# Three of six additions into the residual, from DVE to adding transfers on POOL's queue

## The chip, the cores and the metric

The kernel runs on one core of a Trainium2 chip. The metric is the device time of one execution in microseconds. The core's engines appear as PE (matrix multiplications), DVE (element-wise work on two tensors), ACT (element-wise functions of one tensor), POOL (a second, general engine) and SP (here it only issues transfers). They run side by side and wait for each other through semaphores. Tiles lie in SBUF, 128 partitions wide; matmul results arrive in eight PSUM banks.

## The reference, cut to what matters

Two decoder layers over 256 positions and a model width of 2048, in float32. A layer adds a mixer's output and then a gated feed-forward to the residual:

```
x = x + concatenate([main, mo]) @ w_out[l]
x = x + conv_ffn(rmsnorm(x, g_ffn[l]), w_ffn_up[l], conv_w[l], conv_b[l], w_ffn_down[l])
...
return rmsnorm(x, g_final)

def conv_ffn(h, w_up, cw, cb, w_down):
    a = h @ w_up
    c = causal depthwise convolution of a, width 3, plus cb
    gate, val = c[..., :D_FF], c[..., D_FF:]
    return (silu(gate) * val) @ w_down
```

The inner width D_FF is 5632. What is changed lies in the last line: the product with `w_down` and its addition to the residual.

## The kernel before

**Splits.** Each float32 operand of a matmul is split into a rounded high part and a remainder: ACT writes `whi` (L118 for `w_up`, L709 for `w_down`), DVE writes `wlo` (L119, L710), and PE adds three matmuls per product (L157, L158, L160 for `w_up`, L795 to L797 for `w_down`). Weights come in pieces of 512 KB, issued by SP into four `raw` buffers; `whi` has four buffers, `wlo` five.

**The feed-forward** of a layer runs in three parts of 4, 4 and 3 groups of 512 inner columns. In a part, each group has a gate product and a value product over 16 blocks of the model width (eight chunks each); then two down phases, `ph` 0 and 1, multiply the part's result by `w_down` for the left and the right 1024 output columns. Tokens lie along partitions there: `xt` is the residual, 128 partitions x 2 token blocks x 2048 columns.

**The fast scheme.** Some chunks of a down phase use seven instead of eight block products (a Strassen-like scheme on 2 token blocks x 2 column halves of 512). Four of the products, m1, m5, m6 and m7, have accumulators of their own; the others go straight into the plain accumulators e00, e01, e10, e11. After the last fast chunk, `between` (L1386, ACT) copies the four into a `staged` tile, [128, 2, 4, 512], one set per phase. The plain accumulators are added to `xt` by DVE in `added` (L1407).

**The combine** (`combine`, L1391) later makes the four outputs of the staged products with six DVE operations: two on `staged` itself and four additions or a subtraction into `xt`. For the two phases of the first and second part it is deferred to chunks 2 and 5 of the next part's first gate product. In the third part only phase 0 is fast, and its combine comes right after the first accumulator is added, at the start of phase 1. So a layer has five combines, the program ten.

**Who reads next.** After a deferred combine, `xt` is touched next by the additions of the next part's accumulators. After the last combine of layer 0 (class `Inner`), the additions of e01, e10 and e11, ACT's squares (L1430) and PE's transposes of the first 1024 columns (L406, from `turned`) follow during phase 1; the transposed residual reuses the memory of `staged`. In layer 1 (class `Last`) the additions, the squares (L1499) and the multiplications by the final gain (L1504) follow, and DVE's queue then holds the last weight splits.

**Order.** A scheduler of the framework fixes each engine's order ahead of the run from its own estimates of durations. `keep_in_program_order` holds marked instructions of one engine in the order of the code. The rows of `between` and `combine` follow their data dependences.

Of the kernel before, what the change touches and what calls it, by code (L numbers as in the profile page):

```python
# [13 lines left out]
ALU = mybir.AluOpType  # L14
AX = mybir.AxisListType

P = 128
# [1322 lines left out]
class Tokens:  # L1340
# [48 lines left out]
    def combine(self, ph):  # L1389
        xt, m = self.xt, self.staged[:, ph]  # L1390
        tt = lambda *a: self.k.tc.keep_in_program_order(self.nc.vector.tensor_tensor(*a))  # L1391
        n1, n2 = (slice((2 * ph + i) * 512, (2 * ph + i + 1) * 512) for i in range(2))
        tt(m[:, 2], m[:, 2], m[:, 0], ALU.subtract)
        tt(m[:, 3], m[:, 3], m[:, 2], ALU.add)
        tt(xt[:, 0, n1], xt[:, 0, n1], m[:, 0], ALU.add)
        tt(xt[:, 1, n1], xt[:, 1, n1], m[:, 3], ALU.subtract)
        tt(xt[:, :, n2], xt[:, :, n2], m[:, 1:2].to_broadcast([P, 2, 512]), ALU.add)
        tt(xt[:, :, n2], xt[:, :, n2], m[:, 2:4], ALU.add)

    def deferred(self):  # L1400
        waiting, self.waiting = self.waiting, []
# [155 lines left out]
```

## Time and profile before

| | |
|---|---|
| Median of three runs | 2030.46 us (2029.62 to 2032.41) |
| Profiled execution: span, first to last instruction | 2027.8 us |
| Granted PE clock, mean | 0.999 |
| PE busy | 2017.2 us, 15136 matmuls |
| DVE busy | 1618.2 us, 2433 instructions |
| ACT busy | 1167.1 us |
| POOL busy | 112.8 us |
| Transfers | 409.24 MB, 202 GB/s on average |
| Additions into `xt` by combines (L1391) | 40, from 614.9 to 1997.2 us |

The page gives the profiled execution's span, not its time with what lies around it; the span is 2.7 us below the median of the runs. A row of a timeline gives the start in us, the duration of the merged instructions, engine, line, operation, the tiles written and read, the count, and in brackets the engine's idle time just before and what ended it. A row of a group gives count, then busy us and mean ns, then idle time and its releaser. A row of a window gives, after its length, each engine's busy time with its instructions, then the granted clock, the share of the DMA engines' time that was busy, and GB/s.

### The profile page before, as it was taken

The numbers are of one execution on the slowest core, as the hardware profiler recorded it, in microseconds if no ns is written. First come the engines' busy times: TensorE is split into PE (matmuls) and PEld (weight loads), VectorE is DVE, ScalarE is ACT, GpSimd is POOL, SyncE is SP. The second block draws the span as 40 slices with busy tenths as digits, with TensorE's granted clock in tenths as the row PEclk, the third lists the DMA queues.
The fourth block names the chain that finished last, engine by engine and source line by source line (L and its number), as shares of the span: only waits on it lengthen the run. The fifth ranks groups of instructions, "written<-read, shape, count | busy, mean of one in ns | idle before, by whom it ended". The sixth has DMA issues, their size and how long they took to land.

```text
span 2027.8 us, 38053 instructions
## 1 busy us (share of the span) xinstructions
PE 2017.2 (99%) x15136; PEld 1912.3 (94%) x15136; DVE 1618.2 (80%) x2433; ACT 1167.1 (58%) x1675; POOL 112.8 (6%) x169
## 2 busy tenths in 40 slices
PE   9999999999999999999999999999999999999998
PEld 8989999999889999899989999999988999889996
DVE  6866766778898788987878786777889878898787
ACT  6754744545565555655566675455566555565565
POOL 0000013100000000000002141400000000000000
PEclk9999999999999999999999999999999999999999
DMA  8876556688657676577656634568865767657764
GB/s 255 234 216 181 166 193 195 192 209 259 208 177 218 198 240 199 179 216 246 187 179 187 183 113 162 190 196 210 257 205 181 219 192 246 196 177 219 241 206 145
DMA packets 248263, 409.24 MB, mean 202 GB/s; under 512 B 71502, under 2 KB 78996, under 8 KB 248084
## 3 DMA queue, kind: packets, MB, share of 16 engines
q1 hardware_dynamic: 247892, 406.27, 65.4%
q8 instruction: 118, 1.93, 0.4%
q14 instruction: 61, 0.50, 0.1%
q10 hardware_dynamic: 192, 0.54, 0.1%
HBM read 400.46 MB, written 2.10 MB: 199 GB/s over the span
## 4 chain that ended last, share of the span: by engine, by line
PE 99%; DVE 0%; ACT 0%; issue 0%; ACTq 0%
PE ps L157 22%; PE ps L158 22%; PE ps L160 22%; PE ps L796 7%; PE ps L797 7%; PE ps L795 7%; PE ps L189 2%; PE ps L190 2%; PE ps L191 2%; PE ps L524 1%; PE ps L406 0%; PE ps L604 0%; PE ps L602 0%; PE ps L603 0%; PE ps L1236 0%; PE ps L1024 0%
## 5 line engine op out<-in xcount | busy, mean ns | idle before, releaser
L118 ACT ACTIVATE whi<-raw 128x1024 fp32r<-128x1024 f32 x484 | 512.7, 1061 | 513.1 <-PE ps L158 373.6
L119 DVE TENSOR_TENSOR wlo<-raw,whi 128x1024 fp32r<-128x1024 f32 x484 | 599.0, 1241 | 246.6 <-ACT whi L118 244.1
L157 PE MATMUL ps<-xhl,whi 128*128 128x256 f32 x3264 | 763.1, 277 | 0.0
L158 PE MATMUL ps<-xhl,whi 128*128 128x256 f32 x3264 | 761.5, 276 | 0.0
L158 PEld LDWEIGHTS ps<-xhl,whi 128*128 128x128 f32 x3264 | 612.8, 188 | 0.5
L157 PEld LDWEIGHTS ps<-xhl,whi 128*128 128x128 f32 x3264 | 612.7, 188 | 0.6
L160 PE MATMUL ps<-xhl,wlo 128*128 128x256 f32 x3264 | 436.6, 276 | 0.0
L160 PEld LDWEIGHTS ps<-xhl,wlo 128*128 128x128 f32 x3264 | 400.5, 188 | 0.0
L710 DVE TENSOR_TENSOR wlo<-raw,whi 128x1024 fp32r<-128x1024 f32 x112 | 134.3, 1220 | 31.5 <-ACT whi L709 30.3
L796 PE MATMUL ps<-wlo,h 128*128 128x512 f32 x404 | 157.3, 390 | 0.0
L797 PE MATMUL ps<-whi,h 128*128 128x512 f32 x404 | 157.2, 389 | 0.0
L709 ACT ACTIVATE whi<-raw 128x1024 fp32r<-128x1024 f32 x112 | 115.7, 1055 | 53.1 <-PE ps L158 37.3
L795 PE MATMUL ps<-whi,h 128*128 128x512 f32 x404 | 128.8, 390 | 0.0
L157 PE MATMUL ps<-mainhl,whi 128*128 128x256 f32 x512 | 119.7, 277 | 0.0
L158 PE MATMUL ps<-mainhl,whi 128*128 128x256 f32 x512 | 119.3, 276 | 0.0
L890 ACT ACTIVATE c<-a,cT 128x256 f32<-128x256 f32 x176 | 99.7, 592 | 32.2 <-DVE a L237 30.2
L709 ACT ACTIVATE whi<-xs 128x1024 fp32r<-128x1024 f32 x52 | 53.8, 1059 | 87.3 <-DVE xs L757 73.1
L158 PEld LDWEIGHTS ps<-mainhl,whi 128*128 128x128 f32 x512 | 96.0, 188 | 0.0
L157 PEld LDWEIGHTS ps<-mainhl,whi 128*128 128x128 f32 x512 | 95.9, 188 | 0.0
L795 PEld LDWEIGHTS ps<-whi,h 128*128 128x128 f32 x404 | 75.8, 188 | 15.7
L797 PEld LDWEIGHTS ps<-whi,h 128*128 128x128 f32 x404 | 75.8, 188 | 15.7
L796 PEld LDWEIGHTS ps<-wlo,h 128*128 128x128 f32 x404 | 75.9, 188 | 15.4
(378 smaller groups left out, 2896.6 us busy)
## 6 DMA issues: line engine op xcount, KB each, us to landing
raw<-in_w_ffn_up SPq DMA_DIRECT2D x352, 512.0 KB, 4.4
raw<-in_w_ffn_down SPq DMA_DIRECT2D x126, 512.0 KB, 4.5
raw<-in_w_out SPq DMA_DIRECT2D x64, 512.0 KB, 3.9
raw<-in_w_in_a SPq DMA_DIRECT2D x56, 512.0 KB, 4.2
gate<-in_w_ffn_down SPq DMA_DIRECT2D x38, 512.0 KB, 4.6
raw<-in_w_mem_kv SPq DMA_DIRECT2D x31, 512.0 KB, 4.8
sums<-in_w_ffn_down SPq DMA_DIRECT2D x48, 256.0 KB, 7.1
raw<-in_w_in_b SPq DMA_DIRECT2D x16, 512.0 KB, 4.1
```

The costliest lines, as they stand in the source:

```text
L118: nc.scalar.activation(hi[:, :n], raw[:, :n], AF.Copy)
L119: nc.vector.tensor_tensor(lo[:, :n], raw[:, :n], hi[:, :n].bitcast(F32), ALU.subtract)
L157: mm(acc[:, :S], wh, x[:, :S], start=first, stop=False)
L158: mm(acc[:, :S], wh, x[:, S:], start=False, stop=False)
L160: mm(acc[:, :S], wl, x[:, :S], start=False, stop=last)
L189: mm(acc, xh, wh, start=first, stop=False)
L709: self.behind(self.nc.scalar.activation(hi, w, AF.Copy))
L710: self.behind(self.nc.vector.tensor_tensor(lo, w, hi.bitcast(F32), ALU.subtract))
L795: mm(o, xh, wh, start=start, stop=False)
L796: mm(o, xh, wl, start=False, stop=False)
L797: mm(o, xl, wh, start=False, stop=stop)
L890: nc.scalar.activation(c, a, AF.Identity, scale=w(2), bias=w(3))
```

## The change

In `combine`, both operations on `staged` and the subtraction into `xt` stay on DVE. The other three additions into `xt` become transfers from `staged` to `xt` that add to what they overwrite, issued from POOL's queue in program order: m5 to both token blocks of the second 512 columns (read twice by a broadcast), m1 to token block 0 of the first 512 columns, and the two combined products to both token blocks of the second 512 columns.

```diff
         xt, m = self.xt, self.staged[:, ph]
         tt = lambda *a: self.k.tc.keep_in_program_order(self.nc.vector.tensor_tensor(*a))
         n1, n2 = (slice((2 * ph + i) * 512, (2 * ph + i + 1) * 512) for i in range(2))
+        onto = lambda o, a: self.k.tc.keep_in_program_order(self.nc.gpsimd.dma_start(out=o, in_=a, accum_op=ALU.add))
         tt(m[:, 2], m[:, 2], m[:, 0], ALU.subtract)
         tt(m[:, 3], m[:, 3], m[:, 2], ALU.add)
-        tt(xt[:, 0, n1], xt[:, 0, n1], m[:, 0], ALU.add)
         tt(xt[:, 1, n1], xt[:, 1, n1], m[:, 3], ALU.subtract)
-        tt(xt[:, :, n2], xt[:, :, n2], m[:, 1:2].to_broadcast([P, 2, 512]), ALU.add)
-        tt(xt[:, :, n2], xt[:, :, n2], m[:, 2:4], ALU.add)
+        onto(xt[:, :, n2], m[:, 1:2].to_broadcast([P, 2, 512]))
+        onto(xt[:, 0, n1], m[:, 0])
+        onto(xt[:, :, n2], m[:, 2:4])
```

The lines behind it move down by one (the accumulator addition is L1408 now). The new rows of POOL's queue come in threes. The last combine of layer 0 on POOL, with what stands ahead and behind (in the brackets, DMASW are the semaphores of POOL's transfers, DMAHW those of the others):

```order
L1393 DMA xt_4185<-staged_1352_9421 128x512 [waits Activation_49]
L1393 DMA xt_4185<-staged_1352_9421 128x2x512 [waits DMASW1_49,DVE_49]
L1393 DMA xt_4185<-staged_1734_11802 128x2x512 [waits DMASW4_49,DMASW0_49,Activation_49]
L1393 DMA xt_4185<-staged_1734_11802 128x512 [waits DVE_49,Activation_49]
L1393 DMA xt_4185<-staged_1734_11802 128x2x512 [waits DMASW4_49,DVE_49]
```

The three rows of `staged_1734` are this combine's: the first waits for ACT's copies and earlier transfers, the third for the first (DMASW4) and for DVE. Behind them POOL has only work of the next layer.

DVE around the last combine of layer 1, before (`wlo` are weight splits, `ps_3495`, `ps_3494` and `ps_3496` the accumulators e10, e01 and e11):

```order
L1407 TENSOR_TENSOR xt_15701<-ps_3495_23324,xt_15701 128x512 [waits DVE_49]
L1391 TENSOR_TENSOR xt_15701<-xt_15701,staged_3492_23320 128x2x512 [waits DVE_49]
L710 TENSOR_TENSOR wlo_3577_23711<-raw_3574_23706,whi_3576_23710 128x1024 [waits DMAHW6_49,Activation_49]
L710 TENSOR_TENSOR wlo_3579_23715<-raw_3575_23708,whi_3578_23714 128x1024 [waits DMAHW7_49,Activation_49]
L1407 TENSOR_TENSOR xt_15701<-ps_3494_23323,xt_15701 128x512 [waits DVE_49]
L1407 TENSOR_TENSOR xt_15701<-ps_3496_23325,xt_15701 128x512
L710 TENSOR_TENSOR wlo_3583_23747<-raw_3580_23742,whi_3582_23746 128x1024 [waits DMAHW0_49,Activation_49]
L1504 TENSOR_TENSOR xt_15701<-xt_15701,gb_23321 128x512 [waits Activation_49] x3
L710 TENSOR_TENSOR wlo_3585_23751<-raw_3581_23744,whi_3584_23750 128x1024 [waits DMAHW1_49,Activation_49]
```

And now:

```order
L1408 TENSOR_TENSOR xt_15701<-ps_3495_23324,xt_15701 128x512 [waits DVE_49]
L710 TENSOR_TENSOR wlo_3577_23711<-raw_3574_23706,whi_3576_23710 128x1024 [waits DMAHW6_49,Activation_49]
L1505 TENSOR_TENSOR xt_15701<-xt_15701,gb_23321 128x512 [waits DMASW4_49,Activation_49]
L710 TENSOR_TENSOR wlo_3579_23715<-raw_3575_23708,whi_3578_23714 128x1024 [waits DMAHW7_49,Activation_49]
L710 TENSOR_TENSOR wlo_3583_23747<-raw_3580_23742,whi_3582_23746 128x1024 [waits DMAHW0_49,Activation_49]
L710 TENSOR_TENSOR wlo_3585_23751<-raw_3581_23744,whi_3584_23750 128x1024 [waits DMAHW1_49,Activation_49]
L1408 TENSOR_TENSOR xt_15701<-ps_3494_23323,xt_15701 128x512 [waits DMASW5_49]
L1408 TENSOR_TENSOR xt_15701<-ps_3496_23325,xt_15701 128x512
L1505 TENSOR_TENSOR xt_15701<-xt_15701,gb_23321 128x512 [waits Activation_49] x3
L710 TENSOR_TENSOR wlo_3589_23759<-gate_3586_23754,whi_3588_23758 128x1024 [waits DMAHW2_49,Activation_49]
```

The additions of e01 and e11 stand behind the splits 3583 and 3585 now, and the first of them waits for the third transfer (DMASW5). ACT's splits 3582 and 3584 stand ahead of its squares of these columns now; before, 3584 stood behind them.

PE in layer 0 during phase 1, at the third group of transposes (`ps_1828`), before:

```order
L797 MATMUL ps_1797_12070<-whi_1826_12207,h_1501_10098 128x512
L406 MATMUL ps_1828_12235<-ident_67,xt_4185 128x128 x4
L795 MATMUL ps_1794_12067<-whi_1831_12247,h_1501_10098 128x512 [waits Activation_49]
L796 MATMUL ps_1794_12067<-wlo_1832_12248,h_1501_10098 128x512 [waits DVE_49]
L797 MATMUL ps_1794_12067<-whi_1831_12247,h_1501_10098 128x512
L795 MATMUL ps_1794_12067<-whi_1833_12251,h_1501_10098 128x512 [waits Activation_49]
```

And now:

```order
L797 MATMUL ps_1797_12070<-whi_1826_12207,h_1501_10098 128x512
L795 MATMUL ps_1794_12067<-whi_1831_12247,h_1501_10098 128x512 [waits Activation_49]
L796 MATMUL ps_1794_12067<-wlo_1832_12248,h_1501_10098 128x512 [waits DVE_49]
L797 MATMUL ps_1794_12067<-whi_1831_12247,h_1501_10098 128x512
L795 MATMUL ps_1794_12067<-whi_1833_12251,h_1501_10098 128x512 [waits Activation_49]
L406 MATMUL ps_1828_12235<-ident_67,xt_4185 128x128 [waits DMASW6_49,DVE_49]
L795 MATMUL ps_1795_12068<-whi_1831_12247,h_1501_10098 128x512
L796 MATMUL ps_1795_12068<-wlo_1832_12248,h_1501_10098 128x512
L406 MATMUL ps_1828_12235<-ident_67,xt_4185 128x128 [waits DVE_49]
L406 MATMUL ps_1828_12235<-ident_67,xt_4185 128x128 x2
```

The group comes behind four matmuls that it preceded, its first transpose waits for the third transfer, and two matmuls stand between it and the others.

## The prediction

> **What bounds the kernel now.** I read the page's busy times and chain first, then the waits of TensorE (PE), then the timelines of the two places where the combined products are needed soonest.
>
> ```profile
> span 2027.8 us, 38053 instructions
> PE 2017.2 (99%) x15136; PEld 1912.3 (94%) x15136; DVE 1618.2 (80%) x2433; ACT 1167.1 (58%) x1675; POOL 112.8 (6%) x169
> PE 99%; DVE 0%; ACT 0%; issue 0%; ACTq 0%
> ...
> PE ps L491 <- DVE ones L288: 1.1, 1, 1.1
> PE ps L604 <- DVE pT L246: 0.2, 1, 0.2
> PE ps L796 <- DVE wlo L710: 0.2, 1, 0.2
> ```
>
> PE is busy for 2017.2 of 2027.8 us and is 99% of the chain that ended last. In the whole program it waits for DVE three times, 1.5 us in all, and 1.1 of that is the first microsecond of the program. So DVE, though 80% busy, runs in PE's shadow. Time taken from DVE is worth nothing unless one of these waits shrinks; time by which DVE comes late is paid in full once DVE's lead over PE is used up.
>
> **What the change removes.** The rows are DVE's groups by form, and they carry 40 additions, 20 of each size, in ten combines:
>
> ```profile
> L1391 DVE TENSOR_TENSOR xt<-xt,staged 128x1024 f32<-128x1024 f32 x20 | 24.3, 1216 | 0.0
> L1391 DVE TENSOR_TENSOR xt<-xt,staged 128x512 f32<-128x512 f32 x20 | 13.7, 683 | 0.0
> ```
>
> Each combine loses both additions of 1024 elements a partition and one of the two of 512: 10 x (2 x 1.216 + 0.683) = 31.2 us of DVE, 1.9% of its 1618.2. What stays is the two operations on the staged tile and one subtraction into the residual. Four of a layer's five combines are spread through a gate product in which ACT waits for PE and not the reverse (ACT's timeline at the first two):
>
> ```profile
> 614.23 1.06 ACT L118 ACTIVATE whi<-raw 128x1024 fp32r<-128x1024 f32 x1 [1.78 <-DMA raw<-in_w_ffn_up]
> 616.38 1.07 ACT L118 ACTIVATE whi<-raw 128x1024 fp32r<-128x1024 f32 x1 [1.08 <-DMA raw<-in_w_ffn_up]
> 619.84 1.06 ACT L118 ACTIVATE whi<-raw 128x1024 fp32r<-128x1024 f32 x1 [0.98 <-PE ps L158]
> 622.56 1.06 ACT L118 ACTIVATE whi<-raw 128x1024 fp32r<-128x1024 f32 x1 [1.66 <-PE ps L158]
> ```
>
> From 619.84 on every weight split of ACT waits for PE to free one of the four `whi` buffers, one in 2.72 us. The split at 622.56 takes the buffer of the one at 614.23, four back. Two thirds of a chunk's matmuls read `whi`, so PE began with that one about 1.8 us before 622.5, and it had been ready since 615.3: 5 us of lead at the leanest point. DVE coming earlier gains 0 there.
>
> **What it adds.** Thirty transfers, per combine 512, 256 and 512 KB, issued by POOL. No row of this profile shows a transfer that adds, nor one issued by POOL. The nearest are:
>
> ```profile
> q1 hardware_dynamic: 247892, 406.27, 65.4%
> raw<-in_w_ffn_down SPq DMA_DIRECT2D x126, 512.0 KB, 4.5
> xt<-xs SPq DMA_DIRECT2D x32, 128.0 KB, 5.2
> ```
>
> A plain load of the same 512 KB lands 4.5 us after its issue (lower bound). An adding transfer must also read its destination; if that doubles everything it is 9.0. The only transfers between SBUF tiles, 128 KB in short pieces and issued four at a time, take 5.2; scaled by four that is 20.8, the far upper bound. I take 7 us as D, the time of one 512 KB transfer from issue to landing: between 4.5 and 9.0, nearest the load, which has its size and its row length, and not the short pieces. By the Trainium skill, DMA: Bandwidth & Descriptors, section Anatomy of one DMA — SWDGE (gpsimd) path, a transfer of this path takes 2.0 us plus its bytes over 436 GB/s, which is an estimate of 3.2 us; with it the sum below is the same zero.
>
> **Where an added transfer can be late.** In the regular combines the next reader of these columns is an accumulator addition a whole feed-forward part later. Only the last combine of each layer, in the last part, has near readers. POOL's three rows there (shown with the change) say: the third transfer waits for the first to land, since both write the same columns, and for DVE's sum of products. So it lands at max(sum ready, first issued + D) + D. In layer 1, DVE's additions of the accumulators into those columns (L1407, now L1408) moved behind the splits 3583 and 3585, and the first of them waits for the third transfer. Queued behind them on DVE are three gain multiplications and the splits 3589 and 3591, for which PE waits. The times, from the timelines of ACT, DVE and PE before:
>
> ```profile
> 1985.10 1.57 ACT L1386 ACTIVATE staged<-ps 128x512 f32<-128x512 f32 x3
> 1990.73 0.68 DVE L1391 TENSOR_TENSOR staged<-staged 128x512 f32<-128x512 f32 x1
> 1999.53 1.07 ACT L709 ACTIVATE whi<-raw 128x1024 fp32r<-128x1024 f32 x1 [2.29 <-DVE wlo L710]
> 2000.55 1.28 DVE L1407 TENSOR_TENSOR xt<-ps,xt 128x512 f32<-128x512 f32 x2
> 2001.27 0.63 ACT L1499 ACTIVATE fjunk<-xt 128x512 f32<-128x512 f32 x1 [0.67 <-DVE xt L1407]
> 2002.89 1.88 DVE L1504 TENSOR_TENSOR xt<-xt,gb 128x512 f32<-128x512 f32 x3
> 2006.33 2.01 ACT L709 ACTIVATE whi<-gate 128x1024 fp32r<-128x1024 f32 x2 [2.16 <-PE ps L797]
> 2007.42 2.36 DVE L710 TENSOR_TENSOR wlo<-gate,whi 128x1024 fp32r<-128x1024 f32 x2 [1.52 <-ACT whi L709]
> 2008.70 0.50 PE L796 MATMUL ps<-wlo,hkT 128*128 128x512 f32 x1
> ```
>
> The first transfer's source is ready at 1985.7 (first of the three copies), the product sum at 1991.3. If T is when the third lands, the addition, its ACT square and two more squares end at T + 2.8 (0.72, then 3 x 0.63 and gaps), and ACT must start the split at 2006.33. So T may be up to 2003.5. DVE by its own order comes there near 2002.9: two ACT splits of 1.07 from 1999.53 end 2001.7, plus a split of 1.2. With D = 7, the third lands at max(1991.3, 1992.7) + 7 = 1999.7: 3.8 us to spare. The later reader is covered, so the loss is 0; without that cover it is 2D - 17.8 in layer 1.
>
> In layer 0 the readers are DVE's additions and PE's transposes of the residual. The third group of transposes now stands behind four matmuls of its chunk that it preceded; its first waits for the third transfer, the others for both additions.
>
> ```profile
> 1026.73 1.56 ACT L1386 ACTIVATE staged<-ps 128x512 f32<-128x512 f32 x3
> 1032.51 0.69 DVE L1391 TENSOR_TENSOR staged<-staged 128x512 f32<-128x512 f32 x1
> 1045.07 2.36 DVE L710 TENSOR_TENSOR wlo<-raw,whi 128x1024 fp32r<-128x1024 f32 x2 [0.26 <-ACT whi L709]
> 1049.45 0.60 PE L406 MATMUL ps<-ident,xt 128*128 128x128 f32 x4
> ```
>
> The transposes come at 1049.45 plus four matmuls of 0.23, 1050.3; both additions (1.28 us) must be done, so T may be up to 1049.0. DVE reaches them at 1046.3, after the first split of the pair at 1045.07. First transfer from 1027.3: landing 1027.3 + 14 = 1041.3, 7.7 us to spare; the loss is 0, else 2D - 21.7.
>
> Sum: the profiled span 2027.8, minus 0, plus 0; what lies around a span is not in the page, but the runs' median is 2.7 us above it, so 2030.5. I add 0.5 for small collisions with the loads (next part) and predict **2031.0 us**.
>
> **Rivals.** *Adding transfers that are slow* (the other side). Both layers' thresholds are in D: nothing up to 8.9, then 2D - 17.8 from layer 1, and from 10.9 also 2D - 21.7 from layer 0. At D = 9.0 that is 0.2 us, at 13 it is 8.2 + 4.3 = 12.5 (2043.0), at 20.8 23.8 + 19.9 = 43.7 (2074). For it: nothing here measures such a transfer, the third is serial behind the first, and the engines of the queues are 0.82 and 0.84 busy in the two places (the last two rows; the last columns are DMA share and GB/s). Against it: the loads of 4.5 us run beside the same traffic.
>
> ```profile
> 612.00:618.00 6.00, 6.00 (x55) 6.00 (x55) 6.00 (x8) 2.79 (x4) 0.00 (x0) 1.00 0.91 318
> 618.00:624.00 6.00, 6.00 (x55) 6.00 (x55) 6.00 (x7) 2.98 (x3) 0.00 (x0) 1.00 0.72 216
> 1034.00:1042.00 8.00, 8.00 (x39) 6.57 (x38) 8.00 (x10) 3.83 (x7) 0.00 (x0) 1.00 0.82 306
> 1992.00:2000.00 8.00, 8.00 (x37) 6.61 (x36) 8.00 (x10) 4.27 (x6) 0.00 (x0) 1.00 0.84 328
> ```
>
> *Weight loads crowded out* in the eight regular combines. About 1.25 MB of additions fall into 615 to 625 us, where 9 to 28% of some 310 GB/s is free, 0.7 MB. Counted once they leave a backlog of 2 us, counted twice 6, against the 5 us of lead: up to 1 us each, 8 in all, 2038. I give it less than its arithmetic says since ACT's wait is PE's again from 619.84 on.
>
> *A real gain.* DVE is 6.00 of 6.00 busy there; if PE's waits were DVE's, 31 us would be on offer. The waits show 0.2 us of it, in the last chunk, and that split waits for ACT, which waits for PE. 2030.3.
>
> *Descriptors held up by DVE.* POOL's own operations vary beside DVE:
>
> ```profile
> L279 POOL TENSOR_TENSOR sq<-xT x30: 612/789/1598, 288.7 to 1316.3; 128x256 f32<-128x256 f32 x30
> ```
>
> The same squaring takes 0.61 to 1.60 us. If POOL's preparation of a transfer were held off while DVE runs without a gap, as it does in 1992 to 2000, the third would start only when DVE stops at its addition, 2002.9, and land 4.5 us later at 2007.4: 3.9 us lost in layer 1, none in layer 0, where DVE idles before 1045: 2034.4. The Trainium skill, SBUF — State Buffer, section SBUF: two separate sides, warns of this for DVE operations in a 2-port mode, and for two SBUF inputs only against a GpSimd operation that reads SBUF. The spread of L279, which reads, fits that; whether writing descriptors is hit, no row here shows.
>
> **How the numbers follow.** No change (nothing late, or D below about 11): 0.67. Slow adding transfers beyond that: 0.17. Crowded loads: 0.07. Held descriptors: 0.06. A gain over 0.2%: 0.03. About 0.2%, 4 us, is what a measurement here can tell from none. The held descriptors lie at that edge and are counted as slower. Faster 0.03, same 0.67, slower 0.30. The range goes down to 2028, under the fastest run shown, and up to 2044, where D would be 13.3, which leaves out the slow tail.
>
> **What would show it.** DVE's busy time near 1587 us; PE's waits for DVE still under 2 us; the first L1408 addition that waits for a transfer starting before 1047 and 2004; the DMA list giving the 512 KB transfers 5 to 9 us. Wrong: PE idle near 1050 or 2008 behind a split or a transpose, or ACT waiting for weight loads, near 615 and at the other regular combines, for over 5 us.

## The result and the profile after

The changed kernel takes 2035.64 us (median; 2034.16 to 2037.93) against 2030.26 us before: a ratio of 1.0027 with a 95% interval of 1.0020 to 1.0034, that is 4 to 7 us slower. The profiled execution took 2034.53 us; its span is 4.9 us longer than before.

The head of the page, its chain of waits, and the list of PE's waits:

```profile
span 2032.7 us, 38141 instructions
PE 2018.1 (99%) x15136; PEld 1911.7 (94%) x15136; DVE 1589.9 (78%) x2403; ACT 1166.5 (57%) x1675; POOL 146.5 (7%) x199
PE 86%; issue 9%; DMA 3%; DVE 1%; ACT 1%; POOL 0%; SPq 0%; POOLq 0%; ACTq 0%; DVEq 0%
...
PE ps L406 <- DMA xt<-staged: 1.5, 1, 1.5
PE ps L795 <- ACT whi L709: 1.5, 2, 0.9
PE ps L796 <- DVE wlo L710: 1.2, 3, 0.8
```

DVE is relieved of 28.3 us (1618.2 before). PE does the same work, but there are two new groups of waits, and a third, for DVE's splits, has grown from 0.2 to 1.2 us. The chain, 99% PE before, now holds 9% of "issue" and 3% of transfers from the staged tile. These shares do not measure the loss: the chain follows POOL's queue back to the regular combines, and the "issue" is in the main time in which that queue stood idle between two combines (141.6 us before 1027.68 in the rows further down). The loss is in PE's waits. They are few and short, so the next question is where they stand. DVE's timeline at two points that both kernels have, the first accumulator addition after layer 1's last staging and one of the final gain multiplications, before and then after:

```profile
1982.63 0.68 DVE L1407 TENSOR_TENSOR xt<-ps,xt 128x512 f32<-128x512 f32 x1
2022.08 0.75 DVE L1527 SCALAR_TENSOR_TENSOR xt<-xt,froot,gb 128x512 f32<-128x512 f32 x1
```

```profile
1984.33 0.68 DVE L1408 TENSOR_TENSOR xt<-ps,xt 128x512 f32<-128x512 f32 x1
2027.06 0.75 DVE L1528 SCALAR_TENSOR_TENSOR xt<-xt,froot,gb 128x512 f32<-128x512 f32 x1
```

Up to layer 1's last combine 1.7 us are lost (1984.33 - 1982.63), at the end 5.0 (2027.06 - 2022.08): 1.7 around layer 0's last combine and 3.3 around layer 1's. These are the two places of the prediction. POOL's timeline there, and the time from issue to landing of the three transfers of each (the view of the staged tile, one window for each place):

```profile
1027.68 2.13 POOL L1393 DMA_DIRECT2D xt<-staged  x2 [141.64 <-ACT staged L1386]
1040.75 1.20 POOL L1393 DMA_DIRECT2D xt<-staged  x1 [10.94 <-DMA xt<-staged]
...
1987.94 2.16 POOL L1393 DMA_DIRECT2D xt<-staged  x2 [142.38 <-DVE wlo L710]
2001.06 1.20 POOL L1393 DMA_DIRECT2D xt<-staged  x1 [10.97 <-DMA xt<-staged]
...
DMA to landing us min/median/max: 8.8/12.5/14.1
...
DMA to landing us min/median/max: 7.6/12.5/14.4
```

With three transfers the three numbers are the three of them. The first 512 KB take 12.5 us, the 256 KB issued 1 us later 14 us, and the third, which waits 11 us on POOL for the first, 8.8 and 7.6 us. In layer 0 the readers meet them so (ACT, PE and DVE):

```profile
1042.87 0.63 ACT L1431 ACTIVATE src<-xt 128x512 f32<-128x512 f32 x1 [5.16 <-DMA xt<-staged]
1042.89 0.66 PE L406 MATMUL ps<-ident,xt 128*128 128x128 f32 x4 [1.49 <-DMA xt<-staged]
1049.61 1.29 DVE L1408 TENSOR_TENSOR xt<-ps,xt 128x512 f32<-128x512 f32 x2 [2.08 <-DMA xt<-staged]
```

PE's transposes wait 1.49 us for the *second* transfer, the 256 KB queued behind the first. The third lands at 1049.6, and PE waits for nothing more there. In layer 1:

```profile
2003.09 0.63 ACT L1500 ACTIVATE fjunk<-xt 128x512 f32<-128x512 f32 x1 [5.59 <-DMA xt<-staged]
2004.81 0.74 PE L795 MATMUL ps<-whi,h 128*128 128x512 f32 x2 [0.91 <-ACT whi L709]
2008.72 1.29 DVE L1408 TENSOR_TENSOR xt<-ps,xt 128x512 f32<-128x512 f32 x2 [0.43 <-DMA xt<-staged]
2012.40 0.50 PE L795 MATMUL ps<-whi,hkT 128*128 128x512 f32 x1 [0.58 <-ACT whi L709]
2013.66 0.51 PE L796 MATMUL ps<-wlo,hkT 128*128 128x512 f32 x1 [0.76 <-DVE wlo L710]
```

The second transfer holds ACT's square for 5.59 us; the splits queued behind it on ACT are late, and PE waits 0.91 us for one at 2004.8. Then DVE's additions wait for the third until 2008.7; behind them stand the squares and the last splits, and PE waits at 2012.4 and 2013.7. No wait names the additions themselves: PE waits for a split that stands behind an operation that waits for a transfer.

Why the transfers are long is seen in the windows of the two places, before and then after (the last two columns are the busy share of the 16 DMA engines and GB/s):

```profile
1027.00:1041.00 14.00, 14.00 (x64) 11.53 (x63) 12.18 (x14) 7.22 (x10) 0.00 (x0) 1.00 0.94 332
1987.00:2001.00 14.00, 14.00 (x64) 11.59 (x63) 12.33 (x15) 6.99 (x8) 0.00 (x0) 1.00 0.83 304
2001.00:2009.00 8.00, 7.86 (x35) 6.22 (x34) 6.48 (x9) 4.92 (x9) 0.00 (x0) 1.00 0.00 0
```

```profile
1027.00:1041.00 14.00, 14.00 (x63) 11.60 (x62) 9.22 (x10) 5.60 (x7) 2.38 (x3) 1.00 1.04 282
1987.00:2001.00 14.00, 14.00 (x63) 11.61 (x62) 9.14 (x10) 5.61 (x7) 2.16 (x2) 1.00 1.02 282
2001.00:2009.00 8.00, 6.81 (x29) 4.97 (x28) 4.47 (x5) 3.57 (x5) 1.20 (x1) 1.00 0.84 255
```

Before, the loads alone kept the engines 0.94 and 0.83 busy in the 14 us in which the first two transfers now run. With them the share is 1.04 and 1.02, which is full, and fewer bytes move (282 GB/s for 332 and 304): loads that had ended by 2001 run on beyond it.

The packets of each queue tell how the 12.5 us are made up (queue, packets, MB, share of the 16 engines' time; q1 has the loads, q0 POOL's transfers). The first window begins with the issue at 1027.7, the second with the first packet of q0:

```profile
q1 hardware_dynamic: 362, 1.33, 98.3%
...
q1 hardware_dynamic: 598, 2.17, 61.2%
q0 software_dynamic: 416, 0.79, 45.7%
```

From the issue until 1033.1, 5.4 us, no packet of the adding transfers runs, and the loads hold 98.3% of the engines. Then the first two transfers together get 45.7%, the loads give way to 61.2%, and the 768 KB take 9.2 us. Layer 1 is alike: 4.8 us to the first packet, then 10.0 us at 42.2% of the engines. The third transfer has its first data packet 4.4 and 3.2 us after its issue and lands 4.4 us later.

Full engines alone do not make that wait. In a regular combine the first packet came 2.4 us after the issue at 615.4, with the engines no less full:

```profile
615.40:617.80 2.40, 2.40 (x23) 2.40 (x22) 1.92 (x3) 1.12 (x2) 2.39 (x3) 1.00 1.00 375
```

One thing that differs is how much had just been issued ahead: SP issued four loads of 512 KB between 1025.62 and 1026.99, and five between 1985.63 and 1987.90, but only one every 1.1 to 2.3 us before 615.4. So the first packet may wait for the loads issued before it. The loads differ too (375 GB/s here, 250 in layer 0's last combine), and no run changes either alone, so the reason is not shown.

### The profile page after: what moved, and what is told of

It is laid out like the page before. It is cut to its first block, busy times and chain, and to the rows that moved or that the text cites. A ratio compares the mean times of both kernels' runs of the same rounds, so it can differ in the third digit from the quotient of the medians.

```text
span 2032.7 us, 38141 instructions
## 1 busy us (share of the span) xinstructions
PE 2018.1 (99%) x15136; PEld 1911.7 (94%) x15136; DVE 1589.9 (78%) x2403; ACT 1166.5 (57%) x1675; POOL 146.5 (7%) x199
## 3 DMA queue, kind: packets, MB, share of 16 engines
q0 software_dynamic: 6880, 13.11, 3.6%
## 4 chain that ended last, share of the span: by engine, by line
PE 86%; issue 9%; DMA 3%; DVE 1%; ACT 1%; POOL 0%; SPq 0%; POOLq 0%; ACTq 0%; DVEq 0%
PE ps L157 20%; PE ps L158 20%; PE ps L160 20%; PE ps L795 5%; PE ps L796 5%; PE ps L797 5%; DMA xt<-staged 3%; PE ps L189 2%; PE ps L190 2%; PE ps L191 2%; PE ps L524 1%; PE ps L604 0%; PE ps L406 0%; PE ps L602 0%; PE ps L603 0%
## 5 line engine op out<-in xcount | busy, mean ns | idle before, releaser
L1393 POOL DMA_DIRECT2D xt<-staged x30 | 33.4, 1331 | 1328.1 <-ACT staged L1386 535.4
L795 PEld LDWEIGHTS ps<-whi,h 128*128 128x128 f32 x404 | 75.7, 188 | 16.9 <-ACT whi L709 1.3
```

Source lines behind the costliest of these rows:

```text
L795: mm(o, xh, wh, start=start, stop=False)
```

## The experiments

The theory after the result: the whole loss is made in the last combine of each layer, where transfers land later than near readers need them; the other eight combines cost nothing. Open were which property makes a transfer take 13 us, and which of the three is the costly one. All times stand against runs of the kernel before on the same chip.

**Where: the regular combines alone.** `end` is a new argument of `combine`, true in the call from `added`. The edit, cut to the body of the two branches:

```diff
+        if end:
+            tt(xt[:, 0, n1], xt[:, 0, n1], m[:, 0], ALU.add)
+            tt(xt[:, 1, n1], xt[:, 1, n1], m[:, 3], ALU.subtract)
+            tt(xt[:, :, n2], xt[:, :, n2], m[:, 1:2].to_broadcast([P, 2, 512]), ALU.add)
+            tt(xt[:, :, n2], xt[:, :, n2], m[:, 2:4], ALU.add)
+        else:
+            tt(xt[:, 1, n1], xt[:, 1, n1], m[:, 3], ALU.subtract)
+            onto(xt[:, :, n2], m[:, 1:2].to_broadcast([P, 2, 512]))
+            onto(xt[:, 0, n1], m[:, 0])
+            onto(xt[:, :, n2], m[:, 2:4])
```

> Keeps the adding transfers in the eight combines that lie inside a gate product, and gives the last combine of each layer back to DVE. Theory (the whole loss is made in the last combine of each layer, because its transfers land later than their readers): within 0.5 us of the kernel before, 2030.3 us, although 24 transfers remain and their landing times stay 7 to 15 us; PE's waits for transfers of the residual are gone. Rival (the 24 transfers take DMA time from the weight loads, and PE pays it in small pieces over the whole gate product): 3 to 5 us slower than before, 2033 to 2035, with ACT waiting for weight loads.

Measured: 2029.62 us against 2030.02, ratio 0.9998 (0.9989 to 1.0007). The 24 transfers are as slow as in the changed kernel:

```profile
DMA to landing us min/median/max: 7.9/10.0/13.3
```

Transfers of 8 to 13 us cost nothing where the next reader is a feed-forward part away. And 24.9 us taken off DVE (8 x 3.115) gain nothing either.

**Where: the last combines alone.** The edit is the same with the branches exchanged.

> The other half of the change: only the six transfers of the two last combines, everything else added by DVE. Theory: the full loss, 5.0 to 5.5 us over before (2035.3 to 2035.8), with PE waiting 1.5 us for the second transfer in layer 0, and ACT 5 to 6 us for it in layer 1. Rival (crowding by the regular combines): less than 2 us over before. If both halves lose about 2.5 us, both are at work.

Measured: 2036.43 us, ratio 1.0031 (1.0020 to 1.0043), with PE's wait of 1.6 us for the transfer in layer 0 and ACT's of 5.4 in layer 1. Six of the thirty transfers make the whole loss.

**What makes a transfer long: sharing the queue with its neighbour?** In all combines the 256 KB addition goes back to DVE.

```diff
+        tt(xt[:, 0, n1], xt[:, 0, n1], m[:, 0], ALU.add)
         tt(xt[:, 1, n1], xt[:, 1, n1], m[:, 3], ALU.subtract)
         onto(xt[:, :, n2], m[:, 1:2].to_broadcast([P, 2, 512]))
-        onto(xt[:, 0, n1], m[:, 0])
         onto(xt[:, :, n2], m[:, 2:4])
```

> The 256 KB addition is made by DVE again, so that only two transfers of 512 KB are left in a combine, one strictly after the other. Theory (two transfers on the queue together share the engines, so the first takes 13 us only because the second, issued 1 us later, is mixed with it): the first lands 7 to 9 us after its issue, POOL's wait before the second falls from 11 to about 6, the last addition lands near 2003 to 2004 in layer 1; the time is within 1 us of before, 2030 to 2031.3. Rival (a 512 KB adding transfer takes 13 us by itself in these places, because the loads beside it leave no more): POOL's wait stays near 11 us, the last transfer lands near 2008, and 3 to 4 us are lost, 2033.5 to 2034.5.

Measured: 2036.08 us, ratio 1.0026 (1.0017 to 1.0036). My theory fell: alone on its queue the first transfer is as long. The landing times in the two places, now of two transfers each:

```profile
DMA to landing us min/median/max: 9.4/10.8/12.2
...
DMA to landing us min/median/max: 6.1/9.6/13.2
```

12.2 and 13.2 us for the first, with nothing behind it on the queue; 9.4 and 6.1 for the last. The landing times are those that the rival named; the time is some 2 us above its 2033.5 to 2034.5. (The order of PE and DVE moved too, and the clock fell near the end, see the last section, so the time is no exact measure of the two that are left.)

**The adding itself?** The transfers only copy; order, sizes and queue are the same.

```diff
-        onto = lambda o, a: self.k.tc.keep_in_program_order(self.nc.gpsimd.dma_start(out=o, in_=a, accum_op=ALU.add))
+        onto = lambda o, a: self.k.tc.keep_in_program_order(self.nc.gpsimd.dma_start(out=o, in_=a))
```

> The same thirty transfers in the same order, on the same queue, but each only copies and does not add: the sums of these columns are left out, what is written there is the last source alone. If the adding itself (reading the destination too) makes them slow, the 512 KB transfers take 5 to 6 us instead of 9.6 (median), the queue's share of engine time falls from 3.6% to about 2%, and the loss shrinks from 5.4 to under 2 us. If queue, preparation of descriptors and sharing make them slow, landing times stay within 15% of 9.6 and 13.3 us, and the loss stays at 4.5 to 5.5 us. I lean to the first at half its size: landing 7 to 8 us, loss 2 to 3 us.

Measured: 2030.43 us, ratio 1.0000 (0.9991 to 1.0009). The loss is gone altogether, where 2 to 3 us of it were expected to stay. The row of the queue, and the landing times in the two places:

```profile
q0 software_dynamic: 3680, 13.11, 1.7%
...
DMA to landing us min/median/max: 7.4/9.0/9.4
...
DMA to landing us min/median/max: 7.1/9.7/10.5
```

The adding kernel has 6880 packets and 3.6% of engine time for the same 13.11 MB. So adding about doubles both, and takes the last combines from 7 to 10 us a transfer to 8 to 14. That is the difference between no loss and 5 us: in layer 1 the third copy is issued at 1996.42 and lands near 2003.5, and DVE's addition that reads it starts at 2004.12 without a wait for it. But even a copy takes twice the 4.5 us of a load, so adding is not all of it. A copy waits as long for its first packet: from the issue in layer 0 none runs for 5.2 us. Then the 768 KB of copies take 4.5 us, half the time of adding. Whether the packets or the reading of the destination double the engine time was not separated.

**The form of the source?** Product 1 read twice is replaced by products 0 and 1.

```diff
-        onto(xt[:, :, n2], m[:, 1:2].to_broadcast([P, 2, 512]))
+        onto(xt[:, :, n2], m[:, 0:2])
```

> The first transfer of each combine adds products 0 and 1 from two plain rows in place of product 1 read twice (so another sum is formed); size, place and queue stay. If reading one source row twice makes the first transfer slow, it falls from 13 to 8 or 9 us, POOL's wait before the third in the last combines falls from 11 to 6 or 7, the third lands 4 us earlier, and the loss shrinks to under 2 us. If the form of the source does not matter (what I expect, since a copy in place of an addition already took the time down without touching the source), the first still takes 12 to 13 us there and the loss stays at 5 to 6 us over before.

Measured: 2036.21 us, ratio 1.0030 (1.0019 to 1.0041). The first transfer still takes 12 to 13 us (POOL issues the third 12.4 and 12.9 us after it). The form does not matter for it.

**POOL's queue?** The copying variant, with its first transfer on ACT's queue.

```diff
-        onto(xt[:, :, n2], m[:, 1:2].to_broadcast([P, 2, 512]))
+        self.k.tc.keep_in_program_order(self.nc.scalar.dma_start(out=xt[:, :, n2], in_=m[:, 1:2].to_broadcast([P, 2, 512])))
```

> As the variant that copies without adding (the sums of these columns are left out), with the first transfer of each combine issued on ACT's queue and the other two on POOL's. The two kinds of issue stand at the same ten places. If preparing the transfer on POOL and its queue cost 2 us or more, the 512 KB copies on ACT's queue land in about 5 us where those of POOL took 7.0 (median) and 9.2 in the last combines; if the load beside them sets it, they land in 7 to 9 us as on POOL. I expect 5 to 6. Time: that of before within 1.5 us, since each issue occupies ACT only briefly.

Measured: 2029.50 us, ratio 0.9998 (0.9989 to 1.0007). No landing time is listed for ACT's transfers, but in layer 0 POOL waits for one:

```profile
1027.44 0.60 ACTq L1397 DMA_DIRECT2D xt<-staged  x1
...
1039.77 0.70 POOL L1393 DMA_DIRECT2D xt<-staged  x1 [10.52 <-DMA xt<-staged]
```

12.3 us from ACT's issue to POOL's next, where on POOL's queue no copy of this place took over 9.4. I had expected 5 to 6. The first packet of ACT's transfer came at 1032.6, 5.1 us after its issue, as late as on POOL's queue. So for a copy another queue does not help, and neither POOL's preparation nor its queue makes it long. An adding transfer on another queue was not tried. By the Trainium skill, DMA: Bandwidth & Descriptors, section Issuing engines are not separate DMA queues, transfers started from different engines end on the same 16 DMA engines and interleave there. This case agrees: from 1032.5 to 1037.5 packets of all three ran side by side, the loads with 61.8% of the engines, ACT's transfer with 26.1% and POOL's with 12.9%.

**The loads beside it.** Behind layer 1's last transfer, when the loads have ended, four more of 512 KB follow each other, adding and copying in turn. The body of the edit (`end` as above):

```diff
         onto(xt[:, :, n2], m[:, 2:4])
+        if isinstance(self, Last) and end:
+            copy = lambda o, a: self.k.tc.keep_in_program_order(self.nc.gpsimd.dma_start(out=o, in_=a))
+            onto(m[:, 1::2], m[:, 0::2])
+            copy(m[:, 0::2], m[:, 1::2])
+            onto(m[:, 1::2], m[:, 0::2])
+            copy(m[:, 0::2], m[:, 1::2])
```

> The changed kernel with four more transfers of 512 KB behind layer 1's last one, each waiting for the one ahead, after the weight loads have ended: adding, copying, adding, copying between rows of the staged tile that nobody reads any more. They carry nothing of the result and only measure a transfer with no loads beside it. Theory (a transfer on its own is short; weight loads on the same engines stretch it): adding transfers take 4 to 5.5 us from issue to landing, copies 3 to 4, where beside the loads they took 8 to 13 and 8 to 10. Rival (adding has its price wherever it stands): 7.5 us or more for each addition, copies 5 or more. The order of the last matmuls moves with the extra work, so the time itself (2035 to 2038) tells nothing.

Measured: 2034.63 us, ratio 1.0020 (1.0008 to 1.0031); the time was expected to tell nothing. POOL's timeline (L1393 adds, L1401 copies), and the landing times of the four:

```profile
2009.23 1.20 POOL L1393 DMA_DIRECT2D staged<-staged  x1 [6.61 <-DVE wlo L710]
2014.87 0.76 POOL L1401 DMA_DIRECT2D staged<-staged  x1 [4.44 <-DMA staged<-staged]
2018.29 1.19 POOL L1393 DMA_DIRECT2D staged<-staged  x1 [2.66 <-DMA staged<-staged]
2023.71 0.76 POOL L1401 DMA_DIRECT2D staged<-staged  x1 [4.23 <-DMA staged<-staged]
...
DMA to landing us min/median/max: 3.1/4.5/5.1
```

From one issue to the next 5.6 and 5.4 us for an addition and 3.4 for the copy between them. The landing times are 5.0 and 5.1 us for adding and 3.1 for the first copy; the second, 4.1, ran beside the stores of the output. The window from the issue of the first addition to its first data packet:

```profile
2009.20:2011.00 1.80, 1.80 (x10) 1.49 (x9) 1.61 (x4) 1.71 (x5) 1.20 (x1) 1.00 0.01 1
```

On idle engines the packets begin 1.8 us after the issue and then have 0.95 of the engines until 2014.2. Beside loads that kept the engines 0.83 to 0.94 busy before, the same 512 KB took 12 to 13 us: 5 to the first packet, 7 at less than half of the engines. So the theory is right: the adding transfer on its own is well under my 7 us, and the loads stretch it two and a half times.

**Which transfer: the chain?** In the last combines DVE adds the product read twice, so the two transfers left do not wait for each other. The edit, cut to the branch of the last combines (the other holds the lines of the changed kernel):

```diff
+        if end:
+            tt(xt[:, 1, n1], xt[:, 1, n1], m[:, 3], ALU.subtract)
+            tt(xt[:, :, n2], xt[:, :, n2], m[:, 1:2].to_broadcast([P, 2, 512]), ALU.add)
+            onto(xt[:, 0, n1], m[:, 0])
+            onto(xt[:, :, n2], m[:, 2:4])
```

> In the last combine of each layer DVE adds the product read twice, and only two transfers are left there, of different columns, so none waits for another. Theory (the last transfer is late because it starts 13 us after the first): it is issued when DVE's two operations before it are done, near 1034 and 1994, and lands 9 to 13 us later, near 1043 to 1047 in layer 0 and 2003 to 2007 in layer 1, some 2 to 5 us earlier than in the changed kernel. The planner now puts DVE's accumulator additions of layer 0 ahead of a split, so a part of this can be lost again: 2030.5 to 2033.5. Rival (it is not the chain but each single transfer of 10 us or more that is late for its reader): 2034 or more.

Measured: 2033.28 us, ratio 1.0015 (1.0006 to 1.0024), at the upper end of what was expected. DVE meets the last transfer so:

```profile
1046.52 1.29 DVE L1414 TENSOR_TENSOR xt<-ps,xt 128x512 f32<-128x512 f32 x2 [3.59 <-DMA xt<-staged]
2005.26 1.29 DVE L1414 TENSOR_TENSOR xt<-ps,xt 128x512 f32<-128x512 f32 x2 [3.61 <-DMA xt<-staged]
```

POOL issues it at 1036.81 and 1995.56, later than the 1034 and 1994 expected, since DVE's addition stands in front, and it takes 9.7 us each time. It lands 3.1 and 3.5 us earlier than in the changed kernel, 2 us of the loss go, and 3.4 stay: DVE, whose additions the planner had put ahead of splits, still waits 3.6 us at each place.

**Which transfer: the second?** The 256 KB transfer is issued first.

```diff
+        onto(xt[:, 0, n1], m[:, 0])
         onto(xt[:, :, n2], m[:, 1:2].to_broadcast([P, 2, 512]))
-        onto(xt[:, 0, n1], m[:, 0])
         onto(xt[:, :, n2], m[:, 2:4])
```

> The 256 KB transfer is issued before the first 512 KB one. Theory (queued behind 512 KB it lands 14 us after issue; its readers are PE's first transposes in layer 0 and ACT's square ahead of three splits in layer 1): it lands 7 to 9 us after its issue, near 1036 and 1996, and no engine waits for it; PE's wait of 1.5 us for a transfer goes. The first 512 KB transfer lands where it did or 1 us later, so the last one still lands near 1050 and 2009 and its loss stays: 2032.5 to 2034.5, that is 1 to 3 us better than the changed kernel. Rival (the second transfer was hidden behind the third's lateness anyway): 2035 to 2036.

Measured: 2036.70 us, ratio 1.0036 (1.0022 to 1.0050), above even the rival's number: nothing is gained. The 256 KB are there earlier (ACT's square starts at 1998.7, not 2003.1), but take 9.6 to 9.8 us where 7 to 9 were expected, and ACT still waits for them. The first 512 KB transfer now takes 14.4 us, and the last lands later. ACT and DVE in layer 1:

```profile
1998.70 0.63 ACT L1500 ACTIVATE fjunk<-xt 128x512 f32<-128x512 f32 x1 [3.57 <-DMA xt<-staged]
2009.40 1.29 DVE L1408 TENSOR_TENSOR xt<-ps,xt 128x512 f32<-128x512 f32 x2 [3.43 <-DMA xt<-staged]
```

PE then waits once for 3.1 us instead of several times for under 1. Whatever is first on the queue, the last of the three ends 20 to 24 us after the first is issued, and that sets the loss.

No variant is faster than the kernel before: those that lose nothing equal it, since nothing waits for the time that DVE gains.

## Why the prediction was right or wrong

- *Right: DVE's time is worth nothing.* The regular combines alone take 24.9 us from DVE and give a ratio of 0.9998. DVE's busy time came to 1589.9 against the 1587 named.
- *Right: the regular combines are covered.* The price of 0 held, though ACT's waits for those loads rose from 72.0 to 105.8 us in all. But the sign named for it (ACT waiting for a load for over 5 us) was a poor one: the longest was 6.2 us already before, and is 6.0 after.
- *Wrong: D = 7.* This is the step that failed, "between 4.5 and 9.0, nearest the load". Beside the loads the first transfer takes 12.5 us and the third 7.6 to 8.8, 20.8 us from first issue to last landing in layer 1 (1987.94 to 2008.72) where I had 2 x 7 = 14. On idle engines it is 5.0. So size and row length were the wrong likeness. The prediction had read 0.82 and 0.84 of the engines busy and set it aside because "the loads of 4.5 us run beside the same traffic". That traffic costs the added transfer twice: about 5 us to the first packet, and then 0.42 to 0.46 of the engines for the first two transfers. It is not confined to what the loads left free, 0.06 and 0.17 before; the loads gave way and ran later. What it needs is engine time, 7.3 us of all engines for a combine's three transfers (3.6% of 2032.7, over ten). The prediction made a sum of free shares for the regular combines, where it decides nothing, and none for the last ones. Why the first packet waits so long stays open.
- *Right: the deadlines.* In layer 1 the third transfer had to land by 2003.5, or 2005.2 with the 1.7 us that the kernel was late by then. It lands at 2008.7: a loss of 3.5 us by the prediction's rule, against 3.3 measured. The slow-transfer rival, given 0.17, was thus the true mechanism. Its numbers (12.5 us at D = 13) were too high because it used one D for both links of the chain, and the second link is shorter. In layer 1, too, PE had by then lost 1.2 us (0.91 and 0.28) to the second transfer; the later lateness sets the total.
- *Wrong: only the third transfer was priced.* The second, 256 KB, was taken to be early. Queued 1 us behind the first it takes 14 us and is what PE waits for in layer 0. There the rule for the third gives 1049.6 - 1049.0 = 0.6 us; 1.7 were lost, 1.5 of them in the transposes that read the second. With it out of the way the third takes over in the variant with the small one first. That suggests that the two losses do not add; it is no clean test, since its profiled run also has a stretch of half clock.
- *The estimate by the Trainium skill*, DMA: Bandwidth & Descriptors, section Anatomy of one DMA — SWDGE (gpsimd) path, is 3.2 us and agrees with the copy on idle engines, 3.1 us. It is short by 2 us for adding on idle engines and by 9 us for the first adding transfer beside the loads.
- *A reading that the rows shown do not carry.* ACT's rows at the first two regular combines leave out the split at 617.79, so the "four back" from 622.56 cannot be counted in them; in the whole timeline it comes out as said.
- *Not at work: descriptors held up by DVE.* In layer 1 POOL issues the third transfer as soon as the first lands, at 2001.06, and its data packets begin at 2004.2. DVE does nothing in that wait, and the engines are full (DVE's busy time stands third behind the length):

```profile
2001.10:2003.80 2.70, 2.70 (x13) 1.99 (x11) 0.00 (x0) 0.71 (x3) 1.16 (x1) 1.00 1.02 399
```

On idle engines the packets came after 1.8 us, in which DVE was busy for 1.61. So the wait goes with the traffic and not with DVE.

The forecast of 2031.0 was 4.6 us low. The range held the time because it had been drawn up to a D of 13.3 for the slow-transfer rival, not because the forecast's own mechanism held; that part is luck, and "slower" had 0.30. Most of the signs named as wrong came: PE idle behind splits at 2004.8, 2012.4 and 2013.7 and behind a transpose at 1042.9 (2008 and 1050 had been named), DVE's waiting additions at 1049.6 and 2008.7 in place of before 1047 and 2004, 512 KB in a median of 9.6 us and not 5 to 9.

## What to carry to other kernels

Moving work from a busy engine to transfers pays nothing while that engine runs in another's shadow, and its price is a landing time. Price a new transfer for the very window in which it will run, and not by the median landing time of loads that already hold the engines. Beside loads that fill the engines count the wait for its first packet (3 to 5 us in the last combines here) and then its engine time at the share that it gets (a little under half here). Then give a deadline to the reader of each transfer, the small ones queued behind a large one too; where the reader is far off, as in eight of these ten combines, even 13 us cost nothing.

## What the runs showed of the hardware

Adding between SBUF tiles took 5.0 us for 512 KB on idle engines against 3.1 for a copy, with about twice the packets (6880 and 3680) and engine time (3.6% and 1.7%). Beside the loads of the last combines, adding and copying alike had their first packet only about 5 us after the issue, against 1.8 on idle engines.

I had not expected the clock. In four variants the granted clock fell to half near the end after PE had been only partly busy: for 6.8 us in the variant with the 256 KB addition on DVE, and for 3.4 us in the three with the plain source, with the product read twice on DVE, and with the small transfer first. Windows of 2 us of the first of them (PE busy stands second, the clock third from the right):

```profile
2010.00:2012.00 2.00, 1.44 (x6) 0.67 (x4) 2.00 (x4) 2.00 (x7) 0.00 (x0) 1.00 0.00 0
2012.00:2014.00 2.00, 0.64 (x2) 0.19 (x1) 2.00 (x3) 1.51 (x2) 0.00 (x0) 0.89 0.00 0
2016.00:2018.00 2.00, 2.00 (x6) 1.52 (x6) 0.69 (x1) 0.33 (x1) 0.00 (x0) 0.50 0.00 0
```

and of the changed kernel:

```profile
2010.00:2012.00 2.00, 1.81 (x8) 1.16 (x7) 1.81 (x4) 2.00 (x7) 0.00 (x0) 1.00 0.00 0
2012.00:2014.00 2.00, 0.84 (x3) 0.48 (x3) 1.74 (x3) 1.29 (x2) 0.00 (x0) 1.00 0.00 0
```

With PE busy 2.08 of 4 us the clock was halved, and 6 matmuls went where 10 go in 2 us; with 2.65 of 4 it stayed, and with 2.47 of 4 in the variant with the last combines alone it stayed too. In the first of these PE shows no wait for another engine over 1.23 us there. The Trainium skill, TensorE: Matmul & The Clock Gate, section HAM oscillation — how this bites in real kernels, warns of idle gaps over about 3.4 us; in this variant gaps of about a third of that, close together, were enough. (With the plain source and with the small transfer first, PE had been idle for 2 us at a stretch.) Such a stretch costs some 1.7 to 3.4 us more than the waits that start it (an estimate: 3.4 to 6.8 us at half speed), and so the times of the variants do not follow their waits alone. A single trace of each does not tell how often it comes.
